# Writing the openings of four feed-forward stages out in rounds, with one plain block fewer in three of them

## The chip, the cores and the metric

The kernel runs on one core of a Trainium2 chip. The metric is the device time of one execution in microseconds. TensorE (PE in the profile, its weight loads PEld) multiplies, VectorE (DVE) and ScalarE (ACT) work element by element, GpSimd (POOL) helps them, and SyncE (SP) starts most DMAs. Each engine takes its instructions in the order in which the program issued them.

## What is computed

A trunk of two layers on 512 tokens of width 1024. Each layer is a feed-forward half step, a mixing stage, a second feed-forward half step and a gated embedding; a last norm ends it. The change touches the feed-forward half steps alone:

```python
def rmsnorm(x, g):
    y = x * lax.rsqrt(jnp.mean(x * x, axis=-1, keepdims=True) + EPS)
    return y * g

def swiglu(x, w_gate, w_up, w_down):
    return (jax.nn.silu(x @ w_gate) * (x @ w_up)) @ w_down

for i in range(DEPTH):
    h = h + 0.5 * swiglu(rmsnorm(h, ffn1_norm[i]), ffn1_w_gate[i], ffn1_w_up[i], ffn1_w_down[i])
    ...   # mixing, added to h
    h = h + 0.5 * swiglu(rmsnorm(h, ffn2_norm[i]), ffn2_w_gate[i], ffn2_w_up[i], ffn2_w_down[i])
    ...   # gated embedding, added to h
```

The weights of gate and up are 1024 x 2816, those of down 2816 x 1024.

## The kernel before

Activations lie with features on the 128 partitions and the 512 tokens along the row: `h` is eight row chunks of [128, 512]. Every f32 operand is split into a high part in the reduced format f32r (ACT, a copy) and a low part, the rest (DVE, a subtraction); one product of two operands is three matmuls, high x high, high x low, low x high (`mm3`, L160). A weight chunk is [128, 1024], eight blocks of 128 x 128.

`ffn` (L328) runs four times: FFN1 and FFN2 of layer 0, FFN1 and FFN2 of layer 1. Their first parts, up to the first products, are called the first, second, third and fourth opening below. The 22 column blocks f of gate and up are made in two ways. The first `PLAIN = 4` are plain: gate and up each take one weight chunk and 24 matmuls of 512 columns (`blocks`, L323). The other 18 go by a Strassen-like scheme in seven half-sized products (`p1` to `p7`, L511 to L600; the seven of one f are a unit), each 12 matmuls of 256 columns; their right sides are quarters of the normalised input and four combinations of them, `Th`/`Tl`, which `combined` (L404) makes once while the plain blocks run. Down (`down`, L612) comes after each group of four or five f.

The order is by hand. `item(us, run, tasks)` puts a piece of PE work on a clock of due times; its tasks (loads and splits of weights) are issued `lead` microseconds ahead of it, that is, ahead of the first item whose due time has come (L677). Inside a feed-forward stage every engine's program order is this order. In the opening:

- `chunk_tasks` (L361) loads a weight chunk (18 us ahead) and splits it (12 us ahead, two items early): the high copy on ACT, L376, then the low subtraction on DVE, L131. Raw chunks have two buffers, high and low parts three each, so the high copy of a chunk waits until PE has left the chunk three before it.
- `plain` (L425) issues the 24 matmuls of one chunk, then a step of each generator in `side`: `gated` (L393: DVE, ACT Silu, DVE, ACT, DVE for one f) and `combined` (two ACT copies `pw` L408, two POOL subtractions L411, two DVE operations L414 and L415, the ACT copy `th` L417, the DVE subtraction `tl` L131).
- `Norm.wide` (L223) makes 1/rms of all tokens on every partition at once: two matmuls with ones (L228, L229), then twelve DVE operations on [128, 512]. It stands behind the first chunk (in the first opening behind the fourth), and `gated` needs its result `st.rb`.

`Norm.tok` (L205) and `Norm.bc` (L242) are the other way, used by the mixing and embedding stages: sums of squares by token into [128, 4] (four f32 matmuls, L209, which the trace shows as eight), 1/rms on these four columns (twelve small DVE operations), then four transposes (L245) and one ACT copy (L247) to spread it over the partitions.

The stage ahead of the second and fourth opening is the mixing stage, ahead of the third the embedding stage; there the order of PE is fixed by hand or by program order and the scheduler places the other engines' work, weight splits of the coming opening among it.

Of the kernel before, what the change touches and what calls it, by code (L numbers as in the profile page):

```python
# [17 lines left out]
P = 128  # L18
# [15 lines left out]
PLAIN = 4  # L34
# [59 lines left out]
def trunk(ctx: ExitStack, tc, xT, pT, pos, W, gains, cst, dftc, out):  # L94
# [22 lines left out]
    onesr = cp.tile([P, 1], F32R, name="onesr")  # L117
    S.copy(onesr, ones)
# [61 lines left out]
    class Norm:  # L180
# [24 lines left out]
        def tok(self, by=None):  # L205

            pt = bank("pm")
# [15 lines left out]
        def wide(self, tile):  # L223

            hi, lo = tile("nhi", F32R), tile("nlo", F32R)
            split(hi, lo, self.acc)
            pt = bank("pm")
            mm(pt, onesr.to_broadcast([P, P]), hi, start=True, stop=False)  # L228
            mm(pt, onesr.to_broadcast([P, P]), lo, start=False, stop=True)  # L229
            v, a = tile("nv", F32), tile("na", F32)  # L230
            V.tensor_scalar(v, pt, 1.0 / self.n, EPS, op0=ALU.mult, op1=ALU.add)
            rb = sp.tile([P, T], F32, tag="rbc", name="rbc", bufs=3)
            g = rb.bitcast(I32)
            V.tensor_single_scalar(a.bitcast(I32), v.bitcast(I32), 1, op=ALU.arith_shift_right)
            V.tensor_scalar(g, a.bitcast(I32), -1.0, 1597463007.0, op0=ALU.mult, op1=ALU.add)
            for _ in range(3):
                V.scalar_tensor_tensor(a, rb, -0.5, rb, op0=ALU.mult, op1=ALU.mult)
                V.tensor_tensor(a, a, v, op=ALU.mult)
                V.scalar_tensor_tensor(rb, a, 1.5, rb, op0=ALU.add, op1=ALU.mult)
            return rb  # L240

        def bc(self, r, scale=1.0):  # L242
            pb = bank("pm")
# [79 lines left out]
    def blocks(o, hi, lo, st, base=0):  # L323
        for k in range(NK):
            b = slice((base + k) * P, (base + k + 1) * P)
            mm3(o, hi[:, b], lo[:, b], st.hi[k], st.lo[k], k == 0, k == NK - 1)

    def ffn(l, cgu, cd, st, nxt, first=False):  # L328
# [5 lines left out]
        with tc.tile_pool(name="ap", bufs=1) as ap, tc.manual_schedule():  # L334
# [26 lines left out]
            def chunk_tasks(w, c, halves=False, lead=12.0):  # L361

                if (l, c) in ahead:
                    w["hl"] = ahead.pop((l, c))
                    return []

                def dma():
                    w["raw"] = wp.tile([P, CHUNK], F32, tag="wraw", name="wraw", bufs=2)
                    nc.sync.dma_start(w["raw"], W[l, c])

                def prep():
                    hi = wp.tile([P, CHUNK], F32R, tag="whi", name="whi")
                    lo = wp.tile([P, CHUNK], F32R, tag="wlo", name="wlo")
                    for i in range(1 + halves):
                        b = slice(i * CHUNK // (1 + halves), (i + 1) * CHUNK // (1 + halves))
                        S.copy(hi[:, b], w["raw"][:, b])  # L376
                    lo_of(lo, w["raw"], hi)
                    w["hl"] = hi, lo
# [6 lines left out]
            side = []  # L385
# [7 lines left out]
            def gated(f, ps2):  # L393
# [9 lines left out]

            def combined(i):  # L404

                xg = tile("pw", 6, [2, T])
                for j in range(2):
                    S.activation(xg[:, j], h[:, i + 4 * j], AF.Copy, scale=st.g(i + 4 * j))  # L408
                t = tile("pw", 6, [4, H])
                (b11, b12), (b21, b22) = ((xg[:, j, 0:H], xg[:, j, H:T]) for j in range(2))  # L410
                G.tensor_tensor(t[:, 0], b11, b12, op=ALU.subtract)  # L411
                G.tensor_tensor(t[:, 1], b22, b12, op=ALU.subtract)
                yield True
                V.scalar_tensor_tensor(t[:, 2], t[:, 0], -1.0, b22, op0=ALU.mult, op1=ALU.subtract)  # L414
                V.scalar_tensor_tensor(t[:, 3], t[:, 2], -1.0, b21, op0=ALU.mult, op1=ALU.subtract)  # L415
                hi, lo = tile("th", 4, [4, H], F32R), tile("tl", 4, [4, H], F32R)
                S.copy(hi, t)  # L417
                Th.append(hi)
                Tl.append(lo)
                yield True  # L420
                lo_of(lo, t, hi)

            pairs = []

            def plain(f, i, w):  # L425
                def run():
                    n = 2 * f + i
                    if i == 0:
                        pairs.append((bank("ps"), bank("pm")))
                    blocks(pairs[f][i], *w["hl"], st)  # L430
                    if n == ready:
                        st.rb = st.norm.wide(qd)
                    late = [f] if n > ready else list(range(f + 1)) if n == ready else []
# [1123 lines left out]
```

## Time and profile before

| | us |
|---|---|
| median of 3 runs (2091.53 to 2094.8) | 2092.74 |
| the profiled execution | 2091.12 |
| its span, first to last instruction | 2089.3 |
| PE busy in the span | 2008.6 |
| DVE, ACT, POOL busy | 1567.7, 1016.6, 356.4 |
| mean granted TensorE clock | 0.985 |

The profile is of one execution. A matmul's start is recorded and its end is modelled, so the distance from one start to the next is the better measure of PE's pace. The granted clock has two levels, 1.0 (2.4 GHz) and 0.5 (1.2 GHz); a mean between them is a mixture over the stretch. An idle time in brackets is followed by the instruction that ended it.

### The profile page before, as it was taken

The page shows a single profiled execution, that of the slowest core. Times are in us where ns is not written, and L with a number is a line of the kernel's source. Part 1 is how long each engine was busy: PE and PEld are TensorE (multiplying, and loading weights), DVE is VectorE, ACT ScalarE, POOL GpSimd, SP SyncE. Part 2 cuts the span into 40 slices and gives each one's busy share as a digit, 9 for nine tenths or more (in the row PEclk, how much of TensorE's full clock was granted, in tenths as well). Part 3 has the DMA queues.
Part 4 walks back from the last instruction along what each step waited for, and adds up shares of the span by engine and source line. Part 5 has one row for each costly group of instructions (what it writes and reads, how often), then busy time and mean ns, then how long its engine had stood idle before and what let it go on. Part 6 is the DMA issues. An engine that isn't in the chain of part 4 may idle for free.

```text
span 2089.3 us, 31724 instructions
## 1 busy us (share of the span) xinstructions
PE 2008.6 (96%) x12216; PEld 1770.4 (85%) x12216; DVE 1567.7 (75%) x2607; ACT 1016.6 (49%) x1938; POOL 356.4 (17%) x415
## 2 busy tenths in 40 slices
PE   7899999999999999999999999999989999999997
PEld 5789999888777899998768999988877878999977
DVE  5687787687856778877867887776786667788777
ACT  3534454456734445445544444454675353444463
POOL 0222232001001232221011322220000022233200
PEclk9899999999999999999999999999999999999999
DMA  4365554221123555562225456522210246555431
GB/s 137 102 171 152 151 151 129 83 81 48 57 71 105 147 140 153 152 162 88 94 81 166 134 145 169 152 88 87 83 54 21 91 125 170 145 153 139 138 112 50
DMA packets 96664, 244.23 MB, mean 117 GB/s; under 512 B 10592, under 2 KB 14064, under 8 KB 96512
## 3 DMA queue, kind: packets, MB, share of 16 engines
q1 hardware_dynamic: 73488, 200.98, 28.9%
q0 software_dynamic: 20784, 37.84, 11.2%
q10 hardware_dynamic: 2240, 3.38, 0.5%
q8 instruction: 96, 1.57, 0.3%
q14 instruction: 56, 0.46, 0.1%
HBM read 240.06 MB, written 2.10 MB: 116 GB/s over the span
## 4 chain that ended last, share of the span: by engine, by line
PE 81%; DVE 8%; ACT 5%; issue 3%; DMA 1%; POOL 0%; DVEq 0%; ACTq 0%; POOLq 0%
PE ps L493 29%; PE ps L162 8%; PE ps L161 8%; PE ps L163 7%; PE pm L161 7%; PE pm L163 7%; PE pm L162 7%; PE pm L493 5%; DVE wlo L131 1%; ACT whi L376 1%; ACT pw L408 1%; DVE tl L131 1%; PE ps L718 1%; DVE xl L312 1%; PE ps L719 1%
## 5 line engine op out<-in xcount | busy, mean ns | idle before, releaser
L493 PE MATMUL ps<-th,pw 128*128 128x256 f32 x2304 | 442.9, 284 | 1.5 <-ACT pw L457 1.0
L131 DVE TENSOR_TENSOR wlo<-wraw,whi 128x1024 fp32r<-128x1024 f32 (+3 forms) x275 | 344.4, 1253 | 130.7 <-ACT whi L376 93.6
L493 PEld LDWEIGHTS ps<-th,pw 128*128 128x128 f32 x2304 | 371.6, 193 | 4.4 <-ACT pw L457 1.7
L493 PE MATMUL ps<-tl,pw 128*128 128x256 f32 x1152 | 327.1, 284 | 0.0
L376 ACT CAST whi<-wraw 128x512 fp32r<-128x512 f32 (+1 forms) x261 | 204.4, 811 | 220.9 <-PE pm L162 118.0
L493 PEld LDWEIGHTS ps<-tl,pw 128*128 128x128 f32 x1152 | 221.8, 192 | 1.1
L131 DVE TENSOR_TENSOR pw<-qd,pw 128x512 fp32r<-128x512 f32 x216 | 172.6, 801 | 9.9 <-ACT pw L457 4.8
L469 POOL DMA_DIRECT2D qd<-in_W x144 | 125.9, 963 | 215.2 <-DMA qd<-in_W 212.7
L161 PE MATMUL pm<-ah,whi 128*128 128x512 f32 x392 | 155.3, 396 | 0.0
L163 PE MATMUL pm<-ah,wlo 128*128 128x512 f32 x392 | 154.6, 394 | 0.0
L162 PE MATMUL pm<-al,whi 128*128 128x512 f32 x392 | 154.2, 393 | 0.0
L559 ACT COPY g<-ps 128x256 f32<-128x256 f32 x72 | 26.8, 373 | 231.8 <-PE ps L493 231.8
L134 ACT CAST whi<-wraw 128x1024 fp32r<-128x1024 f32 (+6 forms) x86 | 81.0, 944 | 119.4 <-PE ps L162 53.1
L161 PE MATMUL ps<-xh,whi 128*128 128x512 f32 x288 | 119.2, 414 | 18.8 <-ACT xh L305 13.6
L457 ACT CAST pw<-qd 128x512 fp32r<-128x512 f32 x216 | 124.3, 616 | 0.0
L134 ACT CAST ah<-g 128x256 fp32r<-128x256 f32 x144 | 56.7, 404 | 137.0 <-DVE g L582 130.3
L161 PE MATMUL ps<-ah,whi 128*128 128x512 f32 x312 | 123.3, 395 | 0.0
L163 PE MATMUL ps<-ah,wlo 128*128 128x512 f32 x312 | 123.0, 394 | 0.0
L162 PE MATMUL ps<-al,whi 128*128 128x512 f32 x312 | 122.7, 393 | 0.0
L131 DVE TENSOR_TENSOR pw<-qa,pw 128x512 fp32r<-128x512 f32 x144 | 108.2, 752 | 16.2 <-ACT pw L457 16.2
L163 PE MATMUL ps<-xh,wlo 128*128 128x512 f32 x288 | 117.0, 406 | 3.3 <-DVE wlo L131 3.2
L162 PE MATMUL ps<-xl,whi 128*128 128x512 f32 x288 | 117.3, 407 | 1.4 <-DVE xl L312 1.3
(389 smaller groups left out, 5187.2 us busy)
## 6 DMA issues: line engine op xcount, KB each, us to landing
wraw<-in_W SPq DMA_DIRECT2D x245, 512.0 KB, 3.4
qd<-in_W SPq DMA_DIRECT2D x216, 256.0 KB, 4.2
qd<-in_W POOLq DMA_DIRECT2D x144, 256.0 KB, 4.5
gr<-in_W SPq DMA_DIRECT2D x8, 512.0 KB, 4.0
wraw<-in_W SPq DMA_DIRECT2D x8, 320.0 KB, 2.8
wraw<-in_dftc SPq DMA_DIRECT2D x4, 516.0 KB, 3.3
h<-in_xT ACTq DMA_DIRECT2D x8, 256.0 KB, 4.4
wraw<-in_W SPq DMA_DIRECT2D x4, 408.0 KB, 3.1
```

The source lines that it names most:

```text
L131: V.tensor_tensor(lo, x, hi.bitcast(F32), op=ALU.subtract)
L134: S.copy(hi, x)
L161: mm(o, wh, xh, start=first, stop=False)
L162: mm(o, wh, xl, start=False, stop=False)
L163: mm(o, wl, xh, start=False, stop=last)
L312: V.scalar_tensor_tensor(xl, h[:, m], self.g(m), self.hi[m].bitcast(F32), op0=ALU.mult, op1=ALU.subtract)
L376: S.copy(hi[:, b], w["raw"][:, b])
L408: S.activation(xg[:, j], h[:, i + 4 * j], AF.Copy, scale=st.g(i + 4 * j))
L457: S.copy(p[:, 0], U[u][src])
L469: nc.gpsimd.dma_start(U[u][name], up[:, T:2 * T] if add == "A22" else gate[:, 0:T], accum_op=ALU.add)
L493: mm(U[u][o], x[:, b], y, start=first and i + j == 0, stop=i == 3 and j == 2, skip_group_check=not first)
L559: S.copy(d["g2"], d["B"])
```

## The change

`PLAIN` becomes 3 and `PLAIN0 = 4` is kept for the first opening (`np0` is the one that applies), so in the second to fourth opening the fourth f goes by the Strassen-like scheme. `wide`, its ones and `chunk_tasks` are removed. A class `Chunk` holds one weight chunk with `load`, `high` and `low` as separate steps (each done once), and `tasks` for the later users as before. `tok` and `bc` may be given a PSUM bank, and share one here. `combined` is cut into four: `quarters` (ACT, POOL), `combined` (DVE), `combined_high` (ACT), `combined_low` (DVE). What an item issues is written out: behind the matmuls of chunk n come the high copy of chunk n + 2 and the low subtraction of chunk n + 1 (`beside`), then a part of the combinations, then steps of `gated`. In the second to fourth opening the first two chunks are one item (`opening2`): both blocks over row chunks 0 to 6, then both over row chunk 7. The sum by token follows on PE there, and the broadcast behind chunk 2 (first opening: behind chunks 3 and 4). The core of the diff:

```diff
-PLAIN = 4
+PLAIN = 3
+PLAIN0 = 4
...
-            def chunk_tasks(w, c, halves=False, lead=12.0):
...
-                    for i in range(1 + halves):
...
-                        S.copy(hi[:, b], w["raw"][:, b])
-                    lo_of(lo, w["raw"], hi)
...
-                return [(lead + 6.0, dma), (lead, prep)]
-            ready = 3 if first else 0
+            class Chunk:
+                def load(self):
+                    if self.raw is None and self.hi is None:
+                        self.raw = wp.tile([P, CHUNK], F32, tag="wraw", name="wraw", bufs=2)
+                        nc.sync.dma_start(self.raw, W[l, self.c])
+                def high(self, n=1):
...
+                            S.copy(self.hi[:, b], self.raw[:, b])
+                def low(self):
...
+                        lo_of(self.lo, self.raw, self.hi)
...
+            np0 = PLAIN0 if first else PLAIN
...
-            def plain(f, i, w):
...
-                    if n == ready:
-                        st.rb = st.norm.wide(qd)
...
+            def beside(n):
+                if n + 2 < 2 * np0:
+                    chunks[n + 2].high()
+                if n + 1 < 2 * np0:
+                    chunks[n + 1].low()
+            def opening(n):
+                def run():
+                    plain(n)
+                    beside(n)
+                    i = n - 2
+                    if 0 <= i < 4:
+                        quarters(i)
+                    if 0 <= i - 1 < 4:
+                        combined(i - 1)
+                        combined_high(i - 1)
                     step()
+                    for f in {5: (0, 1), 6: (2,), 7: (3,)}.get(n, ()):
+                        gate(f)
+                    if 0 <= i - 1 < 4:
+                        combined_low(i - 1)
+                    if n == 3:
+                        tok()
+                    if n == 4:
+                        bc()
+            def opening2():
+                for ks in (range(NK - 1), range(NK - 1, NK)):
+                    plain(0, ks)
+                    plain(1, ks)
+                chunks[2].high()
+                chunks[2].low()
+                quarters(0)
+                quarters(1)
                 for i in range(2):
+                    combined(i)
+                    combined_high(i)
+                for i in range(2):
+                    combined_low(i)
+                tok()
+                chunks[3].high()
+            def later(n):
+                def run():
+                    plain(n)
+                    beside(n)
+                    if n == 2:
+                        quarters(2)
+                        quarters(3)
+                    if n in (2, 3):
+                        combined(n)
+                        combined_high(n)
+                    step()
+                    if n > 2:
+                        gate(n - 3)
+                    if n in (2, 3):
+                        combined_low(n)
+                    if n == 2:
+                        bc()
+            loads = lambda n: [(18.0, chunks[n].load)]
...
+                item(11.2, opening2, [(19.0, lambda: (chunks[0].load(), chunks[1].load())), (18.0, prepare)])
+                for n in range(2, 2 * np0):
+                    item(5.6, later(n), loads(n))
```

(`prepare` is `high` and `low` of chunks 0 and 1.)

## Rows read from the trace of the kernel before

**Rows 1.** Windows: busy PE, PEld, DVE, ACT, POOL (instructions), granted clock, DMA share, GB/s.

```profile
30.59:95.70 65.11, 55.04 (x256) 45.55 (x254) 42.59 (x61) 29.75 (x48) 12.12 (x14) 0.87 0.36 97
100.00:360.00 260.00, 260.00 (x1781) 241.34 (x1780) 211.46 (x325) 118.08 (x248) 70.65 (x81) 1.00 0.56 151
626.41:693.18 66.77, 62.16 (x304) 50.17 (x302) 44.64 (x64) 31.71 (x50) 11.18 (x14) 0.97 0.38 111
1046.03:1118.23 72.20, 64.88 (x304) 51.65 (x302) 50.09 (x73) 34.05 (x54) 11.19 (x14) 0.93 0.37 105
1650.72:1718.13 67.41, 63.17 (x303) 51.49 (x302) 44.65 (x64) 31.71 (x50) 11.16 (x14) 0.95 0.39 110
```

**Rows 2.** Timeline, PE, second opening: start, duration, line, out<-in [idle, releaser].

```profile
631.99 0.40 PE L228 MATMUL pm<-qd,onesr 128*128 128x512 f32 x1
...
632.45 0.39 PE L161 MATMUL pm<-xh,whi 128*128 128x512 f32 x1
...
638.02 0.39 PE L161 MATMUL ps<-xh,whi 128*128 128x512 f32 x1
```

**Rows 3.** Chain that ended last, 693 to 703 us: start, length, what.

```profile
693.34 8.62 PE ps L493 x72
```

**Rows 4.** Timeline, DVE, second opening.

```profile
632.65 0.69 DVE L231 TENSOR_SCALAR qd<-pm 128x512 f32<-128x512 f32 x1 [1.25 <-PE pm L229]
...
640.12 0.69 DVE L239 SCALAR_TENSOR_TENSOR rbc<-qd,rbc 128x512 f32<-128x512 f32 x1
```

**Rows 5.** Timeline, ACT, second opening.

```profile
641.56 0.63 ACT L396 ACTIVATE qa<-qa 128x512 f32<-128x512 f32 x1 [9.58 <-DVE qa L395]
...
657.58 1.05 ACT L417 CAST th<-pw 128x1024 fp32r<-128x1024 f32 x1 [3.28 <-DVE pw L415]
...
665.20 1.05 ACT L417 CAST th<-pw 128x1024 fp32r<-128x1024 f32 x1 [3.88 <-DVE pw L415]
```

**Rows 6.** Groups by line, shapes apart, 640 to 676 us, ACT then DVE: busy, mean ns.

```profile
L408 ACT ACTIVATE pw<-h,gv 128x512 f32<-128x512 f32 x8 | 5.3, 713 | 0.0
L376 ACT CAST whi<-wraw 128x1024 fp32r<-128x1024 f32 x5 | 5.2, 1031 | 0.0
...
L131 DVE TENSOR_TENSOR wlo<-wraw,whi 128x1024 fp32r<-128x1024 f32 x5 | 6.1, 1225 | 14.3 <-ACT whi L376 14.3
...
L415 DVE SCALAR_TENSOR_TENSOR pw<-pw 128x256 f32<-128x256 f32 x4 | 1.7, 425 | 0.1
```

**Rows 7.** Timeline, POOL, second opening.

```profile
646.41 0.75 POOL L411 TENSOR_TENSOR pw<-pw 128x256 f32<-128x256 f32 x1 [128.09 <-ACT pw L408]
```

**Rows 8.** Timeline, PE, start of the third opening.

```profile
1051.48 0.51 PE L162 MATMUL ps<-xl,whi 128*128 128x512 f32 x1 [0.54 <-DVE xl L312]
...
1054.23 0.79 PE L161 MATMUL ps<-xh,whi 128*128 128x512 f32 x1 [2.01 <-ACT xh L305]
```

**Rows 9.** Timeline, PE, around a sum by token and a broadcast in other stages.

```profile
441.01 0.95 PE L209 MATMUL pm<-ones,sqacc 128*128 128x1 f32 x8
441.82 0.48 PE L161 MATMUL ps<-xh,whi 128*128 128x512 f32 x1
...
999.36 0.62 PE L245 MATMUL pm<-cs,rtok 128*128 128x128 f32 x4
999.74 0.48 PE L161 MATMUL pm<-whi 128*128 128x512 f32 x1
```

**Rows 10.** Timeline, DVE, the twelve small steps of a 1/rms by token.

```profile
1009.33 0.15 DVE L213 TENSOR_SCALAR var<-pm 128x4 f32<-128x4 f32 x1
...
1011.51 0.16 DVE L177 SCALAR_TENSOR_TENSOR rtok<-rs_a,rs_y 128x4 f32<-128x4 f32 x1
```

**Rows 11.** The page, part 6: DMA issues, KB each, median us to landing.

```profile
qd<-in_W POOLq DMA_DIRECT2D x144, 256.0 KB, 4.5
```

**Rows 12.** Windows: a stretch with both of Rows 9's kinds, and one with idle PE.

```profile
442.00:454.00 12.00, 12.00 (x55) 9.73 (x55) 11.16 (x30) 9.79 (x16) 0.00 (x0) 1.00 0.13 44
665.00:675.00 10.00, 8.48 (x29) 6.11 (x29) 6.13 (x9) 5.31 (x7) 4.01 (x5) 0.83 0.56 127
```

More of the change, by code (lines that the diff above doesn't have):

```diff
@@ L221, in tok, with bc @@
             return r
[L223 to L243, printed above, removed]
+        def bc(self, r, scale=1.0, pb=None):
+            pb = bank("pm") if pb is None else pb
             for c in range(NT):
@@ L321, in bc, with blocks @@
             self.rb = self.norm.bc(self.rt)
-    def blocks(o, hi, lo, st, base=0):
-        for k in range(NK):
+    def blocks(o, hi, lo, st, base=0, ks=range(NK)):
+        for k in ks:
             b = slice((base + k) * P, (base + k + 1) * P)
@@ L419, in combined @@
-                Tl.append(lo)
-                yield True
-                lo_of(lo, t, hi)
-            pairs = []
-            def plain(f, i, w):
-                def run():
[L427 to L430, printed above, removed]
-                    if n == ready:
-                        st.rb = st.norm.wide(qd)
-                    late = [f] if n > ready else list(range(f + 1)) if n == ready else []
-                    step()
-                    i0 = n - (2 if first else 1)
-                    if 0 <= i0 < 4:
-                        side.append(combined(i0))
-                        next(side[-1])
-                    if i == 0 or n == ready:
-                        for x in late:
-                            side.append(gated(x, pairs[x]))
-                            next(side[-1])
-                return run
@@ L446, in ffn, with combined @@
-            for f in range(PLAIN):
-                for i in range(2):
-                    w = {}
-                    tasks = chunk_tasks(w, cgu + 2 * f + i)
-                    item(5.6, plain(f, i, w), tasks)
+            def combined(i):
+                xg, t = xgs.pop(i), ts[i]
+                V.scalar_tensor_tensor(t[:, 2], t[:, 0], -1.0, xg[:, 1, H:T], op0=ALU.mult, op1=ALU.subtract)
+                V.scalar_tensor_tensor(t[:, 3], t[:, 2], -1.0, xg[:, 1, 0:H], op0=ALU.mult, op1=ALU.subtract)
@@ new lines, in combined_high, with combined_low, gate, tok @@
+            def combined_high(i):
+                Th.append(tile("th", 4, [4, H], F32R))
+                S.copy(Th[i], ts[i])
+            def combined_low(i):
+                Tl.append(tile("tl", 4, [4, H], F32R))
+                lo_of(Tl[i], ts.pop(i), Th[i])
+            def gate(f):
+                side.append(gated(f))
+                next(side[-1])
+            pairs = []
+            chunks = [Chunk(cgu + n) for n in range(2 * np0)]
+            norm_bank = []
+            def tok():
+                norm_bank.append(bank("pm"))
+                st.rt = st.norm.tok(pt=norm_bank[0])
@@ new lines, in ffn, with prepare @@
+            loads = lambda n: [(18.0, chunks[n].load)]
+            if first:
+                for n in range(2 * np0):
+                    item(5.6, opening(n), loads(n))
+            else:
+                def prepare():
+                    for n in range(2):
+                        chunks[n].high()
+                        chunks[n].low()
+                item(11.2, opening2, [(19.0, lambda: (chunks[0].load(), chunks[1].load())), (18.0, prepare)])
+                for n in range(2, 2 * np0):
+                    item(5.6, later(n), loads(n))
@@ L521, in run @@
                     step()
-                return run, chunk_tasks(U[u]["gate"], cgu + 2 * u, True, 10.1)
+                return run, U[u]["gate"].tasks(2, 10.1)
             def p5(u):
@@ L638, in ffn @@
             SL = 1.434
-            put(SL, p1(PLAIN))
-            put(SL, p5(PLAIN))
-            put(SL, p2(PLAIN))
+            put(SL, p1(np0))
+            put(SL, p5(np0))
+            put(SL, p2(np0))
             g, f0 = 0, 0
-            for u in range(PLAIN, NF - 1):
-                prev = u - 1 if u > PLAIN else None
+            for u in range(np0, NF - 1):
+                prev = u - 1 if u > np0 else None
                 put(SL, p6(u))
```

76 lines of the change are left out of this document (41 added, 35 removed).

## The prediction

> **What bounds the kernel now.** I read the windows first, then PE's timeline in the stretches where it loses time, then the timelines of the engines that it waits for there. PE is the bound: in a steady feed-forward stretch it is busy for 260.00 of 260.00 us, with DVE at 211 and ACT at 118 [rows 1]. A plain block of 24 matmuls takes 5.57 us (632.45 to 638.02) and the two matmuls of `wide` 0.46 (631.99 to 632.45) [rows 2]; 72 half-width matmuls take 8.62, so a product of twelve takes 1.44 [rows 3]. The other stretches of [rows 1] are the four openings, each from its first plain matmul (the first opening: from its third block, since the blocks before that wait for the inputs) to the end of the second `p2`, nine products in. PE's own work there is 8 x 5.57 + 0.46 + 9 x 1.437 = 57.95 us (first: 6 blocks, 46.81). What is above that is lost: 65.11 - 46.81 = 18.3 in the first opening, 66.77 - 57.95 = 8.8 in the second, 72.20 - 57.95 = 14.3 in the third, 67.41 - 57.95 = 9.5 in the fourth, together 50.8 us [rows 1].
>
> **Why it is lost there.** Two things. `wide` holds DVE from 632.65 to 640.81 [rows 4], and ACT, in order, sits 9.58 us before a Silu that needs its result [rows 5], with the high copy of a later weight chunk queued behind. After that the laps are too long: from one `th` copy to the next takes 665.20 - 657.58 = 7.62 us [rows 5] against 5.57 for the block, because ACT and DVE pass the work to and fro. The lap, by the mean times [rows 6]: two `pw` copies 1.43, high copy 1.03, low part 1.22, `tl` 1.22 (same shape), two operations of L415's kind 0.85, `th` 1.05 [rows 5], 6.8 in all, and the gating of one f makes up the rest. DVE idles 14.3 us in that stretch for the high copies alone [rows 6]: neither engine is full, the order is the bound. The third opening also waits at its start for the last row chunks, 2.01 us in one place [rows 8], and half clock follows the idle: 0.83 granted over ten microseconds is 1.7 us of PE time [rows 12].
>
> **The change part by part.**
>
> *1/rms by token.* It takes twelve wide DVE steps (8.2 us [rows 4]) off and puts twelve small ones there, 1009.33 to 1011.67, 2.3 us [rows 10]. PE pays: 0.81 for the sum (441.01 to 441.82) and 0.38 for the transposes (999.36 to 999.74) [rows 9], less 0.46 for `wide`: +0.73 each, four times +2.9 us. It adds one wait on PE: the transposes stand ahead of the next block in PE's queue and need DVE's last small step. ACT gets one copy of 512 columns (at most the 0.71 of L408 [rows 6]), one more link ahead of the first gate.
>
> *Rounds.* In the new order the low part of chunk n + 1 needs a high copy that ACT made a round earlier, so the lap is cut in two. I count the second opening from its first plain matmul. PE: two blocks to 11.1, the sum to 11.9, block 2 to 17.5, transposes to 17.9, block 3 to 23.5, block 4 to 29.0, block 5 to 34.6. ACT first has a high copy and the last row chunk's two copies (to about 2.3, at the prices of [rows 6]), then the quarters 0 and 1 to 5.1; POOL takes 1.5 for each pair [rows 7]; the two `th` copies end near 8.4, the lows near 9.7. DVE then stands before the sum, which comes at 11.9, and the small steps end at 14.3, wanted at 17.5: 3.2 to spare. The low part of chunk 3 comes at 15.5, wanted (third matmul of its block) at 18.4; chunk 4's behind the third combination at 19.8, wanted at 24.0; chunk 5's at 24.0, wanted at 29.5; the first Strassen chunk's at 27.9, wanted at 34.6. So nothing is late, and the cover is 3 to 7 us; where it is gone, each microsecond costs one. The high copy of chunk 3 waits for block 0, whose last use is now three matmuls from the end of the pair (10.4 instead of 5.6): it lands at 11.5, long before 17.9. In the first opening the same counting leaves 3 us for the transposes and over 4 for the later chunks. The gating there starts two blocks later (behind chunk 5) and shares DVE with the last splits: about 5.1 us of DVE work in that round by the prices of [rows 6], against 5.57.
>
> *Loads.* Raw chunks keep two buffers, so on SP's queue the load of chunk 5 waits for the low part of chunk 3 (15.5), and the first Strassen operand S1 is queued behind it. S1 lands at about 20 and POOL's accumulating DMA behind it at 25 to 26, with 4.5 for each [rows 11]; wanted at 30. That is 4 us of cover; POOL's two subtractions for quarters 3 are issued before it.
>
> *Two blocks share their row chunks.* No matmul is added. In the third opening row chunk 6 is still in the first sweep: PE is there 18 matmuls in, at 1050.2, and its second matmul, due at 1050.4, began at 1051.48 [rows 8]; this 1.0 us stays. Row chunk 7, there at 1054.2 [rows 8], is now wanted at about 1056.9: hidden. But ACT's combinations start some 6 us later than in the second opening, so that the small steps end about when block 2 does, and chunk 3's low part may be a few tenths late. I put 2 us for this opening, 0.5 for each other, 3.5 in all. The bounds: nothing, or, where the scheduler puts the quarters' four copies (2.9 us [rows 6]) ahead of the last row chunk on ACT, 1.0 + 2.9 + 1.7 for the clock [rows 12], 5.6 in that opening.
>
> *One plain block fewer.* Two blocks, 11.14 us, become seven products, 10.06: -1.08, three times -3.2 us. The added unit's splits and loads lie beside PE as those of the steady stretch do, where PE loses nothing [rows 1]; at worst they cost what one lap is too long, 7.62 - 5.57 = 2.05 each [rows 5].
>
> *The start.* One tiny ACT copy (the ones) goes; PE waits for inputs there, so nothing, within two copies either way (1.4 [rows 6]).
>
> **The sum.** Losses 50.8 + 3.2 - 2.9 = 51.1 at most; less 3.5 left over: 47.6. The profiled execution took 2091.12 (span 2089.3 and 1.8 around it) and becomes 2043.5; the median of the runs shown is 1.6 above it, so I predict 2045.
>
> **The rivals.**
>
> *The laps stay.* If ACT and DVE still wait for each other once a round, four rounds of each opening run at 7.62 instead of 5.57: 8.2 each, 32.8 in all, and the gain is 51.1 - 32.8 = 18.3: 2074. For it: the chain quarters, POOL, DVE, ACT, DVE is as long as before. Against: only its own last step waits for all of it; the weight splits no longer do, and the lists above have 3 to 7 us of cover.
>
> *The third opening stays stuck.* Its start keeps the 5.6 worked out above, the transposes wait a further 2 or so in the three openings where DVE has the combinations ahead of them: about 11 left over, 2053. For it: there ACT gets the last row chunks late; against: row chunk 7 has 2.7 us.
>
> *The clock falls at the small matmuls.* The trace keeps 1.00 over a stretch with a sum by token and four transposes [rows 12]. The Trainium skill, page "TensorE: Matmul & The Clock Gate", section "Part 4: PE-mode transpose", says that a transpose does not count as PE work in the same way and that full clock does not engage for it; each opening now has four of them. By that rule a half-clock stretch would follow in each opening; the trace disagrees [rows 12]. One stretch of half clock in each, like the one of 1.7 us in [rows 12], would give 4 x 1.7 = 6.8 more: 2052.
>
> *Slower.* The same mechanism, if PE stayed at half clock from the sum by token to the last plain block: four blocks of 5.57 in each opening take twice as long, 4 x 22.3 = 89 more: 2092.7 - 51.1 + 89 = 2131. It decides from 51.1 / 4 = 12.8 us at full-clock pace run at half in each opening. Against it: 1.00 in [rows 12], and 0.87 at the lowest over a whole opening even with today's waits [rows 1].
>
> **How the numbers follow.** Forecast (2041 to 2050) 0.72; third opening stuck 0.10; laps stay 0.10; clock falls once per opening 0.03; slower 0.03; no change, the laps longer than before, 0.02. About 0.2% (4 us) is what a measurement of this kernel can tell from no change. Faster 0.95, same 0.02, slower 0.03. The range runs from 2039 (all of the 51.1, and the start's 1.4 on the good side) to 2062: it takes in the forecast, the stuck opening and the clock, 0.85, and part of the way to the laps; 2074 is left out.
>
> **What would show it.** Right: between `wide`'s old place and the first product no PE idle over 0.5 us but at the third opening's row chunk 6; windows from the first plain matmul to the second `p2` of 6 x 5.57 + 1.19 + 12.93 = 47.5 us, plus 0.5 to 2, in the second to fourth opening; the granted clock 1.00 there. Wrong: PE waits before the transposes or for low parts, ACT idle of several microseconds before `th` with high copies behind it, or Strassen operands S1 that land late.

## The result, and the profile after

The changed kernel took 2042.28 us (median of 4 runs, 2039.42 to 2044.95), the kernel before 2093.34 beside it (2091.53 to 2094.8). The ratio is 0.9767, 95% interval 0.9753 to 0.978, so about 49 us faster by the ratio; the two medians lie 51.1 us apart. 2045 had been forecast, with 2039 to 2062 as the range. The profiled execution of after is the slowest of its four, 2044.95 with a span of 2043.2. One execution in the whole study, the profiled one of `subs_on_dve` below, ran at 1.28 us a 512-column matmul from start to end instead of 0.232, so it stands in no comparison, and only durations of DVE and what ran beside them are read from its trace.

The openings of after, as windows (busy PE, PEld, DVE, ACT, POOL with instructions, granted clock, DMA share, GB/s). They answer [rows 1], and the second to fourth now end at the second `p2` of a stage that has one plain f less:

```profile
29.21:78.18 48.97, 48.18 (x265) 41.35 (x264) 35.99 (x58) 28.99 (x46) 11.61 (x14) 1.00 0.48 130
611.79:659.53 47.74, 47.74 (x266) 41.25 (x264) 37.89 (x57) 28.89 (x46) 12.89 (x15) 1.00 0.54 152
1024.25:1073.86 49.61, 48.40 (x266) 41.04 (x265) 41.57 (x65) 30.22 (x47) 12.23 (x15) 1.00 0.52 145
1615.18:1662.65 47.47, 47.47 (x265) 41.06 (x264) 37.90 (x57) 28.48 (x45) 13.23 (x15) 1.00 0.55 150
```

The forecast for the second to fourth was 47.5 plus 0.5 to 2 at a clock of 1.00. In the second and fourth PE is busy for every microsecond of the window. Against [rows 1], less the 10.06 us of the seven products that the later unit moves out of the window, the gains are 65.11 - 48.97 = 16.1, 66.77 - 47.74 - 10.06 = 9.0, 72.20 - 49.61 - 10.06 = 12.5 and 67.41 - 47.47 - 10.06 = 9.9, together 47.5 us; 47.6 had been forecast. By opening the forecast was 17.1, 8.7, 12.7 and 9.4 (the loss there, less 0.73, plus 1.08 where a plain f goes, less what I left over). The rest of the span gave 47.5 - (2089.3 - 2043.2) = 1.4 back. The stretch before the first opening became 1.4 shorter (30.59 to 29.21) and the long stretches between and after the openings together 2.8 longer, for reasons that I have not followed.

The waits of PE in the first and the third opening (engine, line, releaser: us, times, longest) are all that the two windows list; in the second and fourth there is none:

```profile
PE ps L562 <- ACT g L628: 0.8, 1, 0.8
...
PE pm L225 <- DVE rtok L176: 1.1, 1, 1.1
```

The laps of ACT in the second opening, which answer [rows 5]:

```profile
617.66 1.05 ACT L415 CAST th<-pw 128x1024 fp32r<-128x1024 f32 x1 [1.25 <-DVE pw L411]
619.00 1.05 ACT L415 CAST th<-pw 128x1024 fp32r<-128x1024 f32 x1 [0.29 <-DVE pw L411]
...
630.37 1.05 ACT L415 CAST th<-pw 128x1024 fp32r<-128x1024 f32 x1 [3.71 <-DVE pw L411]
...
634.70 1.05 ACT L415 CAST th<-pw 128x1024 fp32r<-128x1024 f32 x1 [0.17 <-DVE pw L411]
```

The laps of before are gone: the copies come in pairs, 1.3 and 4.3 us apart. In before there are three laps between the four copies, 7.02, 7.62 and 7.02 us; the first and the last copy, with those of [rows 5] between them, are:

```profile
650.56 1.05 ACT L417 CAST th<-pw 128x1024 fp32r<-128x1024 f32 x1 [2.74 <-DVE pw L415]
...
672.22 1.05 ACT L417 CAST th<-pw 128x1024 fp32r<-128x1024 f32 x1 [3.28 <-DVE pw L415]
```

DVE's idle for high copies of weight chunks, 14.3 us in [rows 6], is 1.9 us from 611.79 to 646.6:

```profile
L130 DVE TENSOR_TENSOR wlo<-wraw,whi 128x1024 fp32r<-128x1024 f32 x5 | 6.1, 1222 | 1.9 <-ACT whi L360 1.9
```

One thing in the trace I had not counted. The small steps of 1/rms, 2.3 us in [rows 10], took 4.4 us here, 623.92 to 628.35. First DVE's timeline, then POOL's, then ACT's, of the same microseconds:

```profile
624.72 0.16 DVE L174 TENSOR_TENSOR rs_a<-rs_a,var 128x4 f32<-128x4 f32 x1
624.92 0.75 DVE L176 SCALAR_TENSOR_TENSOR rs_y<-rs_a,rs_g 128x4 f32<-128x4 f32 x1
625.70 0.66 DVE L173 SCALAR_TENSOR_TENSOR rs_a<-rs_y 128x4 f32<-128x4 f32 x1
...
628.18 0.17 DVE L176 SCALAR_TENSOR_TENSOR rtok<-rs_a,rs_y 128x4 f32<-128x4 f32 x1
...
624.90 0.74 POOL L404 TENSOR_TENSOR pw<-pw 128x256 f32<-128x256 f32 x1 [6.73 <-ACT pw L401]
625.60 0.75 POOL L405 TENSOR_TENSOR pw<-pw 128x256 f32<-128x256 f32 x1
...
624.11 2.56 ACT L401 ACTIVATE pw<-h,gv 128x512 f32<-128x512 f32 x4
```

Each of four steps that met a subtraction of POOL ended when that subtraction did: 624.92 + 0.75 = 625.67 beside 624.90 + 0.74 = 625.64, and 625.70 + 0.66 = 626.36 beside 625.60 + 0.75 = 626.35. ACT's copies are not what holds them: they run from 624.11, and the steps from there to 624.88 still take 0.16 to 0.17 us. In the third opening the chain took 4.3 us, 1038.81 to 1043.06, and PE waited for it.

### The profile page after: what moved, and what is told of

It reads as the page before. It is cut to its first block, busy times and chain, and to the rows that moved or that the text cites. A ratio compares the mean times of both kernels' runs of the same rounds, so it can differ in the third digit from the quotient of the medians.

```text
span 2043.2 us, 32106 instructions
## 1 busy us (share of the span) xinstructions
PE 1987.2 (97%) x12364; PEld 1767.7 (87%) x12364; DVE 1571.1 (77%) x2630; ACT 1027.4 (50%) x1967; POOL 373.0 (18%) x430
## 4 chain that ended last, share of the span: by engine, by line
PE 86%; DVE 7%; ACT 3%; issue 2%; DMA 1%; POOL 0%; DVEq 0%; ACTq 0%; POOLq 0%; SPq 0%
PE ps L562 30%; PE ps L161 8%; PE ps L160 8%; PE ps L162 8%; PE pm L160 7%; PE pm L161 7%; PE pm L162 7%; PE pm L562 5%; DVE wlo L130 1%; DMA wraw<-in_W 1%; DVE xl L292 1%; PE ps L787 1%; PE ps L789 1%; PE ps L788 1%; DVE sqacc L198 1%
## 5 line engine op out<-in xcount | busy, mean ns | idle before, releaser
L562 PE MATMUL ps<-th,pw 128*128 128x256 f32 x2400 | 457.4, 283 | 0.9 <-ACT g L628 0.8
L130 DVE TENSOR_TENSOR wlo<-wraw,whi 128x1024 fp32r<-128x1024 f32 (+6 forms) x272 | 344.5, 1267 | 76.0 <-ACT whi L133 37.9
L562 PEld LDWEIGHTS ps<-th,pw 128*128 128x128 f32 x2400 | 384.6, 191 | 2.6 <-ACT g L628 1.0
L562 PE MATMUL ps<-tl,pw 128*128 128x256 f32 x1200 | 339.2, 283 | 0.0
L562 PEld LDWEIGHTS ps<-tl,pw 128*128 128x128 f32 x1200 | 229.6, 191 | 1.1
L130 DVE TENSOR_TENSOR pw<-qd,pw 128x512 fp32r<-128x512 f32 x225 | 181.0, 804 | 14.9 <-ACT pw L526 9.7
L130 DVE TENSOR_TENSOR pw<-qa,pw 128x512 fp32r<-128x512 f32 x150 | 114.5, 763 | 13.2 <-ACT pw L526 13.2
L160 PE MATMUL ps<-xh,whi 128*128 128x512 f32 x264 | 107.8, 409 | 12.4 <-ACT xh L285 11.7
L562 PE MATMUL ps<-xh,pw 128*128 128x256 f32 x600 | 119.9, 283 | 0.0
L573 POOL TENSOR_TENSOR g<-g,c 128x256 f32<-128x256 f32 x75 | 65.0, 867 | 282.3 <-ACT g L572 282.3
```

The costliest lines, as they stand in the source:

```text
L130: V.tensor_tensor(lo, x, hi.bitcast(F32), op=ALU.subtract)
L160: mm(o, wh, xh, start=first, stop=False)
L562: mm(U[u][o], x[:, b], y, start=first and i + j == 0, stop=i == 3 and j == 2, skip_group_check=not first)
L573: G.tensor_tensor(d["g2"], d["g2"], d["c22"], op=ALU.mult)
```

## The experiments

Each is timed against the kernel before, on the chip that it ran on. To set them side by side, each ratio is turned into a difference from 2092.74 us:

| kernel | median, us | ratio, 95% interval | difference, us |
|---|---|---|---|
| the change | 2042.28 | 0.9767 (0.9753 to 0.978) | -48.8 |
| token_only | 2075.72 | 0.9924 (0.9907 to 0.9942) | -15.9 |
| plain3_only | 2107.96 | 1.0079 (1.0064 to 1.0094) | +16.5 |
| token_plain3 | 2088.87 | 0.9992 (0.9982 to 1.0001) | -1.7 |
| wide_back | 2067.24 | 0.9886 (0.9871 to 0.99) | -23.9 |
| plain4 | 2054.06 | 0.9828 (0.9814 to 0.9841) | -36.0 |
| plain4_late | 2052.02 | 0.9812 (0.9798 to 0.9827) | -39.3 |
| one_each | 2050.55 | 0.9807 (0.9793 to 0.982) | -40.4 |
| one_each_old | 2062.24 | 0.986 (0.9846 to 0.9875) | -29.3 |
| low_two | 2047.06 | 0.9786 (0.9768 to 0.9805) | -44.8 |
| apart | 2044.43 | 0.9782 (0.9769 to 0.9795) | -45.6 |
| quarters_early | 2040.26 | 0.9764 (0.9751 to 0.9778) | -49.4 |
| subs_on_dve | 2039.88 | 0.9758 (0.9743 to 0.9773) | -50.6 |

### One part alone, in the old order

**token_only**: the kernel before with 1/rms by token.

```diff
...
-                        st.rb = st.norm.wide(qd)
+                        norm_bank.append(bank("pm"))
+                        st.rt = st.norm.tok(pt=norm_bank[0])
+                    if n == ready + 1:
+                        st.rb = st.norm.bc(st.rt, pb=norm_bank[0])
...
```

The start of each f's gating moves with it, behind the broadcast.

> The kernel before with 1/rms by token alone: sum behind the first chunk (first opening: the fourth), broadcast one chunk later, gates behind that; four plain blocks, order otherwise as before. Theory (two causes, the wide steps and laps of ACT and DVE that are too long): laps start some 5 us earlier, so about half of each opening's loss goes, and 2.9 us of PE are added: 2075 (2068 to 2082). Rival (the wide steps were the whole cause): all but the 6.6 us at the start of the third opening goes, 2052.

Measured: 15.9 us off, a third of the whole. The laps stay: in the second opening `th` copies of ACT stand 8.15, 7.62 and 7.03 us apart. The middle one:

```profile
647.51 1.05 ACT L419 CAST th<-pw 128x1024 fp32r<-128x1024 f32 x1 [3.88 <-DVE pw L417]
655.13 1.06 ACT L419 CAST th<-pw 128x1024 fp32r<-128x1024 f32 x1 [3.88 <-DVE pw L417]
```

So `wide` was one cause and the laps another, as the prediction had it.

**plain3_only** and **token_plain3**: the same edit of the number of plain f, on the kernel before and on `token_only`.

```diff
-PLAIN = 4
+PLAIN = 3
+PLAIN0 = 4
...
-            for f in range(PLAIN):
+            np0 = PLAIN0 if first else PLAIN
+            for f in range(np0):
...
```

> The kernel before with three plain blocks in the second to fourth opening and nothing else. Theory (the combinations are bound by the laps of ACT and DVE, not by the number of blocks): PE comes to the first product that needs them two blocks earlier and waits there; slower by 3 to 6 us in each of three openings: 2105 (2100 to 2112). Rival (the swap is worth its PE time wherever it is made): 3.2 us faster, 2090.

> The kernel before with 1/rms by token and three plain blocks in the second to fourth opening; order as before, first two blocks apart. What is left to the changed kernel is the rounds and the shared row chunks. Theory: the combinations still come at laps of about 7.6 us and are wanted two blocks earlier, so the swap gains nothing: 2078 (2070 to 2085). Rival (the parts add up): 3.2 below the kernel with the sum by token alone.

Measured: 16.5 us slower alone, and beside 1/rms by token it takes back 14 of the 15.9 us. With two blocks less the late operands meet the products: PE's waits of `plain3_only` from 650 to 690 us, the window of its nine products behind the blocks, and the waits of `token_plain3` (of each kernel's four waits the two longest; the 4.9 us lie ahead of the window):

```profile
PE ps L495 <- ACT whi L377: 4.9, 1, 4.9
PE ps L495 <- DVE tl L132: 2.1, 1, 2.1
```

```profile
665.92:688.80 22.88, 18.17 (x108) 17.06 (x109) 16.42 (x24) 10.32 (x21) 5.20 (x6) 0.68 0.63 150
```

```profile
PE ps L498 <- ACT pw L462: 2.6, 1, 2.6
PE ps L498 <- DVE tl L132: 2.1, 1, 2.1
```

Nine products need 12.93 us [rows 3]; here they take 22.88, part of it idle, and the granted clock is 0.68 over the window. I had the direction of the first. For `token_plain3` I had said that the edit gains nothing; it costs 14 us, and the time came out 11 us above what was expected and outside its range: 22.85 us for the same nine products of its second opening (657.27 to 680.12), at a granted clock of 0.78. Each tenth of clock missing there is 2.3 us of PE.

### One part taken back out of the change

**wide_back**: the change with `wide` in place of the sum by token and the broadcast.

```diff
...
-                tok()
+                st.rb = st.norm.wide(qd)
                 chunks[3].high()
...
```

> The changed kernel with 1/rms of all tokens at once (wide) in the place of the sum by token, and no broadcast behind it. Theory (the twelve wide DVE steps, 8.2 us, stand in front of the low part of chunk 3, in the first opening of chunk 5): low part of chunk 3 about 3.6 us late in the second and fourth opening, about 6 in the third, of chunk 5 about 3.7 in the first; less 0.73 per opening for PE and the waits that are there now: 2055 (2052 to 2060). Rival (the order of the rounds alone does it, DVE has room for the wide steps): PE saves 4 x 0.73, 2039.

Measured: 24.9 us slower than the change, twice what I had counted. PE's wait in the second opening and DVE ahead of it:

```profile
628.29 1.11 DVE L238 SCALAR_TENSOR_TENSOR qd<-rbc 128x512 f32<-128x512 f32 x1
...
636.39 1.22 DVE L132 TENSOR_TENSOR wlo<-wraw,whi 128x1024 fp32r<-128x1024 f32 x1
...
637.66 0.74 PE L164 MATMUL pm<-xh,wlo 128*128 128x512 f32 x1 [5.00 <-DVE wlo L132]
```

The low part of chunk 3 stands behind the twelve wide steps. Four of those ran beside POOL at 1.11 to 1.12 us instead of 0.69, so they took 9.8 us where [rows 4] gave 8.2, and half clock follows the wait (a granted clock of 0.75 from 637.66 to 644.45 in the second opening). The block behind `wide` lost 5.9, 6.8 and 7.1 us in the first, second and fourth opening; in the third it lost 6.7, and 5.5 more went at `wide` and in the block ahead. `wide` costs more here than in the old order (24.9 us against 15.9). That this is because a low part is made one block ahead of its use, not two, is argued from the order and was not run by itself.

**apart**: the first two blocks one after the other.

```diff
-                for ks in (range(NK - 1), range(NK - 1, NK)):
-                    plain(0, ks)
-                    plain(1, ks)
+                plain(0)
+                plain(1)
```

> The changed kernel with the first two blocks of the second to fourth opening one behind the other, over all eight row chunks each. Theory: only the third opening waits for row chunk 7, about 2.7 us, and gives back the 1.5 that it now waits before and behind the transposes; the others don't change: 2043.5 (2042 to 2046). Rival (the shared sweep is what took the third opening's start loss of 6.6 us): 2049.

Measured: 3.2 us above the change by the ratios, whose intervals overlap, near the first of the two expectations. In the third opening PE waits for the last two row chunks again, 2.0 us for one and 0.3 for the other:

```profile
PE ps L160 <- ACT xh L285: 2.0, 1, 2.0
```

**low_two**: the low part of a weight chunk in the round of its high copy.

```diff
                 if n + 2 < 2 * np0:
                     chunks[n + 2].high()
-                if n + 1 < 2 * np0:
-                    chunks[n + 1].low()
+                    chunks[n + 2].low()
...
                 chunks[3].high()
+                chunks[3].low()
```

> The changed kernel with the low part of a chunk made in the same round as its high copy, two chunks ahead, instead of one chunk ahead. Reason given in the prediction (the low part one round behind the high copy is what cuts the lap): laps go back towards 7.6 us, 2 us a round, 2055 to 2070. Rival (the lap is cut by the rest: no wide steps, gates behind the combinations, combinations in parts): DVE waits a little for each high copy and nothing reaches PE, 2042.3 within 2.

Measured: 2047.06, 4 us above the change by the ratios, whose intervals overlap, and not the 2055 to 2070 that the prediction's reason asked for, nor within 2 of 2042.3 as the other expectation had it. `th` copies come 1.34 and 4.74 us apart (617.83 and 619.17, 631.67 and 636.41). So the low part's being a round behind its high copy is not by itself what cut the laps, and `one_each` and `one_each_old` below find what did.

**plain4** and **plain4_late**: four plain f everywhere; `plain4` begins the gating of the fourth f behind chunk 6, `plain4_late` behind chunk 7 (the edit shown is that of `plain4_late`).

```diff
-PLAIN = 3
+PLAIN = 4
...
-                    if n > 2:
-                        gate(n - 3)
+                    for f in {3: (0,), 4: (1,), 5: (2,), 7: (3,)}.get(n, ()):
+                        gate(f)
```

> The changed kernel with four plain blocks in all openings (gates of f = 0 to 3 behind chunks 3 to 6). Theory (in the new order neither form leaves PE waiting, so the swap is worth its PE time): 3 x 1.08 us slower, 2045.5 (2044 to 2047.5). Rival (the fewer blocks are themselves what took waits away): 2050 or more.

> The changed kernel with four plain f everywhere, and the gating of the fourth begun behind the last block (chunk 7) instead of behind chunk 6. In plain4 the nine products after each of the second to fourth opening took 14.4 us instead of 12.9: at 656 us ACT's copy for the last f's activations stood ahead of its copy for the second Strassen operand. Theory: that order is the cause, and with it mended three more plain blocks cost 3 x 1.08 = 3.2 us alone: 2045.5 (2044 to 2048), nine products in 12.9 to 13.1 us in the second to fourth opening. Rival: the products are late behind eight blocks whatever the order: 2050 or more, as plain4 had it (2054).

Measured: 12.8 and 9.5 us above the change, where 3.2 was counted for three swaps. A part of `plain4` was of my making. Its ACT, at the end of the second opening's blocks, and the product that waited:

```profile
655.95 0.62 ACT L394 CAST ah<-qa 128x512 fp32r<-128x512 f32 x1 [3.91 <-DVE qa L392]
656.48 0.61 ACT L526 CAST pw<-qd 128x512 fp32r<-128x512 f32 x1
...
657.14 0.39 PE L562 MATMUL ps<-th,pw 128*128 128x256 f32 x1 [0.54 <-ACT pw L526]
```

The copy `ah` of the last f needs the last block and stands ahead of the copy of a product's operand. With the gating one round later that copy comes first, 4 us ahead of the last block's end (658.43):

```profile
654.33 0.61 ACT L526 CAST pw<-qd 128x512 fp32r<-128x512 f32 x1
...
660.31 0.62 ACT L394 CAST ah<-qa 128x512 fp32r<-128x512 f32 x1
```

and the 1.5 us that the nine products lost in each opening are gone, though the medians moved by 2 to 3 us only. In the traces of the change and of `plain4_late` the six blocks more (33.4 us) and the three shorter stretches of products (29.7 us) make 3.7 of the 9.6 us between the spans. The other 5.9 lie outside, in the stages between and at the end, where half clock is granted for longer (49 us in all against 38, at most 5 us of PE). Why is open. The price of the three plain f more is 3.7 by these stretches, where 3.2 was counted, and 8 to 10 by the medians of `one_each` and `plain4_late`.

### What cut the laps

**one_each**: `plain4_late` with the combinations one a round, as before; the low part of a weight chunk stays a round behind its high copy. **one_each_old**: the same, with the low part in the round of its high copy, which is the old order.

```diff
...
+                    if 0 <= n - 3 < 4:
+                        combined_low(n - 3)
+                    if 0 <= n - 2 < 4:
+                        combined(n - 2)
+                        combined_high(n - 2)
                     step()
+                    if 0 <= n - 1 < 4:
+                        quarters(n - 1)
...
```

> plain4_late, but in the second to fourth opening the four combinations are made one a round as in the kernel before (quarters i, a round later combination i and its high copy, a round after that its low part, each behind the next weight chunk's low part on DVE); the low part of a weight chunk stays one round behind its high copy. Theory of the prediction (the low part a round behind its high copy is what cuts the laps): no lap is over 5.57 us, PE loses nothing in the blocks: 2045 to 2048, as plain4_late. Rival (making the combinations two at once, with their low parts in the same round, is what cut them): laps near 7.6 us again, one to four of them showing in each of three openings: 2055 to 2070.

> one_each, with the low part of a weight chunk in the round of its high copy (two chunks ahead), which is the kernel before's order of combinations and splits in the second to fourth opening; 1/rms by token and the shared row chunks stay. Theory (either of the two parts alone cuts the laps, both gone bring them back): a lap of high copy 1.03, low 1.14, low of a combination 1.14, two operations 0.85, its high copy 1.05, two quarter copies 1.3 and a gating's two copies 1.1 = 7.6 us, 2.05 over a block, over four rounds, less what the head start covers: 4 to 8 us for each of three openings over plain4_late: 2057 to 2070, with th copies 7.6 us apart. Rival (the order of splits and combinations is not what set the laps; 1/rms by token and the shared row chunks did it all): as plain4_late, 2045.5.

Measured: `one_each` equals `plain4_late` (0.9807 and 0.9812), PE loses nothing in its second opening. `one_each_old` is 11 us slower than `one_each`. ACT's copies of the second opening, `one_each` and then `one_each_old` with one row of its DVE and the waits of its PE:

```profile
630.89 1.05 ACT L415 CAST th<-pw 128x1024 fp32r<-128x1024 f32 x1 [0.74 <-DVE pw L411]
...
635.96 1.04 ACT L415 CAST th<-pw 128x1024 fp32r<-128x1024 f32 x1
...
641.30 1.05 ACT L415 CAST th<-pw 128x1024 fp32r<-128x1024 f32 x1 [1.06 <-DVE pw L411]
```

```profile
635.94 1.05 ACT L415 CAST th<-pw 128x1024 fp32r<-128x1024 f32 x1 [3.27 <-DVE pw L411]
...
644.38 1.06 ACT L415 CAST th<-pw 128x1024 fp32r<-128x1024 f32 x1 [3.28 <-DVE pw L411]
...
651.92 1.05 ACT L415 CAST th<-pw 128x1024 fp32r<-128x1024 f32 x1 [3.28 <-DVE pw L411]
...
648.68 1.23 DVE L130 TENSOR_TENSOR wlo<-wraw,whi 128x1024 fp32r<-128x1024 f32 x1 [3.19 <-ACT whi L360]
```

```profile
PE ps L555 <- DVE wlo L130: 1.3, 1, 1.3
...
```

With both gone the laps are back, 8.4 and 7.5 us, and DVE idles 3.2 us for the high copy, then works off `wlo`, `tl` and two operations while ACT idles 3.3. With the low part a round behind, DVE starts at once and the lap is 5.1 and 5.3. With two combinations at once and their low parts in the same round (`low_two`) there are half as many laps. In the second to fourth opening either one is enough; the change has both. (`low_two` has three plain f there, the other kernels of this comparison four.) In the second and fourth opening `one_each_old` takes as long as `token_only`, 62.75 and 62.88 us, 63.45 and 63.05, from the first plain matmul to the second `p2`, so the two parts account there for what the order gives.

The first opening is another matter. `one_each_old` has the low part in the round of its high copy there too, and in every kernel written in rounds the first opening makes one combination a round; yet it is as short as in the change. Its windows, `token_only` and then `one_each_old`, counted as in [rows 1]:

```profile
28.05:86.15 58.10, 51.54 (x265) 43.94 (x264) 37.05 (x61) 29.72 (x48) 12.62 (x14) 0.91 0.38 109
...
28.93:77.42 48.49, 47.95 (x266) 41.26 (x265) 38.02 (x58) 29.09 (x46) 12.85 (x14) 1.00 0.45 131
```

Of the 16.1 us that the first opening gained, 1/rms by token gives 65.11 - 58.10 = 7.0, and about 9 come from the rest of the new order. In the rounds a combination's low part stands in the round of its own high copy and the gating starts one chunk later than in `token_only`; whether one of these or something else in the order does it, no run shows.

### Small steps beside POOL

**quarters_early**: quarters 2 and 3 issued in the first item, ahead of the sum by token.

```diff
...
                 quarters(1)
+                quarters(2)
                 for i in range(2):
                     combined(i)
                     combined_high(i)
+                quarters(3)
...
```

> The changed kernel with the quarters 2 and 3 made ahead of the sum by token (second to fourth opening), so that no POOL subtraction runs beside the small DVE steps. Theory (a small DVE step with two operands in SBUF waits out a POOL subtraction: 0.66 us each instead of 0.16): the steps take 2.4 us in all three openings instead of up to 4.4, and PE's wait of 1.2 us before the transposes of the third opening goes: 2040.8 (2039.5 to 2042.5). Rival (the steps are slow for another reason): steps of 0.66 stay, 2042.3.

Measured: 2040.26, not told apart from the change. In the second opening, where no subtraction runs beside the small steps, the chain takes 2.3 us, and in the fourth as well. Its first and last step in the second:

```profile
621.89 0.16 DVE L212 TENSOR_SCALAR var<-pm 128x4 f32<-128x4 f32 x1 [1.76 <-PE pm L208]
...
624.07 0.16 DVE L176 SCALAR_TENSOR_TENSOR rtok<-rs_a,rs_y 128x4 f32<-128x4 f32 x1
```

In the third opening PE still waits 0.83 us before the transposes. POOL's subtractions only met other work of DVE there (the two `tl` parts took 2.89 us together, where two of 1.22 follow each other elsewhere, and two other small steps became slow):

```profile
1032.95 2.89 DVE L130 TENSOR_TENSOR tl<-pw,th 128x1024 fp32r<-128x1024 f32 x2
...
1035.95 0.52 DVE L167 TENSOR_SCALAR rs_i<-var 128x4 int32<-128x4 int32 x1
1036.50 0.67 DVE L169 TENSOR_SCALAR rs_g<-rs_i 128x4 int32<-128x4 int32 x1
```

**subs_on_dve**: the subtractions of quarters 2 and 3 on DVE, behind the small steps.

```diff
...
-                        quarters(2)
-                        quarters(3)
+                        quarters(2, False)
+                        quarters(3, False)
                     if n in (2, 3):
+                        differences(n, V)
                         combined(n)
...
```

> The changed kernel, but the four subtractions for quarters 2 and 3 in the second to fourth opening run on DVE, ahead of the two operations that need them, instead of on POOL. Theory: the small 1/rms steps took 4.4 us (second opening) and 3.8 us (third) instead of 2.3 because POOL's subtractions ran beside them; with POOL idle there every step takes 0.15 to 0.2 us again, the chain 2.3 to 2.5 us, and PE's wait before the transposes of the third opening (1.23 us) and the 0.36 us behind it go: 2040.6 (2039 to 2043), for DVE has 1.7 us more in that round but spare time. Rival: the steps are slow for another reason (the PSUM read, the ACT copies beside them): they stay at 0.65 us beside ACT's copies, the wait stays, 2042.3.

Measured: 2039.88, the lowest of all; its interval overlaps that of the change, so a gain of 1.8 us is not shown. Its trace agrees with the mechanism. One group of small steps over the whole program (busy, mean ns), first of this kernel, then of the change:

```profile
L176 DVE SCALAR_TENSOR_TENSOR rs_y<-rs_a,rs_g 128x4 f32<-128x4 f32 x14 | 2.3, 162 | 0.5
```

```profile
L176 DVE SCALAR_TENSOR_TENSOR rs_y<-rs_a,rs_g 128x4 f32<-128x4 f32 x14 | 3.9, 281 | 0.4
```

No small step is slow where POOL does not read beside it. This trace alone would not settle it, since ACT has no work beside the small steps of its openings either; the change's own rows and `quarters_early` do. Whether PE's wait in the third opening goes with it can't be read from that execution.

## Why the prediction was right, step by step

*What bounds the kernel, and the 50.8 us.* Right. The second and fourth opening now lose nothing, and the gain in the four windows is 47.5 of the 47.6 forecast.

*1/rms by token.* The direction and PE's price held: 0.81 and 0.36 us for the two groups of small matmuls. DVE's price was mis-sized: the small steps took 4.4 us, not the 2.3 of [rows 10], because those rows stand where POOL is idle and the new place is beside its subtractions. The low part of chunk 3 ended at 629.5, 17.7 after the start of the window instead of 15.5, wanted at 18.5. About 0.8 us was left of the cover that I had put at 2.9, so nothing was lost in the second and fourth opening. The forecast of 3 to 7 us of cover was too good.

*Rounds.* The outcome was right, the reason half of it. "In the new order the low part of chunk n + 1 needs a high copy that ACT made a round earlier, so the lap is cut in two": `one_each` shows that this is enough. `low_two` shows that it is not needed, because the change also makes the combinations two at once. I had the pair in my own count (both `th` copies ended near 8.4, the lows near 9.7; in the trace 8.3 and 9.5) and did not see that it cuts the laps as well. Neither accounts for the first opening, where about 9 us went by the order without them; that part of the forecast came out without its reason. The lap of 7.62 that I priced was also the longest of before's three, 7.02, 7.62 and 7.02, so the rival's four rounds at 7.62 were priced too high.

*Loads.* Nothing came late, but most of the cover that I had counted went. S1 landed 22.3 us after the start of the second opening instead of 20, and POOL's accumulating DMA behind it, one of three with a median of 6.9 us there instead of 4.5, at 29.0 instead of 25 to 26. That is 1 us ahead of the 30 that I had put and 3.9 ahead of ACT's copy, which began at 32.9.

*Third opening.* The sum of 2 us was right (49.61 less 47.5), its places were not, so that the sum agrees is luck. The 1.0 us at row chunk 6 did not come: its low part landed 4.3 us after the opening's start, where PE could go on only after 5.45 in before [rows 8]. DVE's batch of six low parts ahead of it began 3.4 us before the opening instead of 2.3. Before, then after:

```profile
1043.77 4.06 DVE L312 SCALAR_TENSOR_TENSOR xl<-h,gv,xh 128x512 fp32r<-128x512 f32 x6
...
1020.87 4.06 DVE L292 SCALAR_TENSOR_TENSOR xl<-h,gv,xh 128x512 fp32r<-128x512 f32 x6
...
1027.79 0.75 DVE L292 SCALAR_TENSOR_TENSOR xl<-h,gv,xh 128x512 fp32r<-128x512 f32 x1
```

PE, due there at 1028.6, did not stop. Instead 1.1 us went at the transposes, a sign that the text had given to a rival, 0.3 at the low part of chunk 3 behind them, and 0.4 in the products:

```profile
1043.11 0.65 PE L225 MATMUL pm<-cs,rtok 128*128 128x128 f32 x4 [1.06 <-DVE rtok L176]
```

*First opening.* 16.1 against 17.1. The 1.3 us that its products lose at 72.3 us wait for an ACT copy behind the last f's gating, the same order that `plain4` showed; I had said that nothing is late there.

*One plain block fewer.* -3.2 was the price with every operand in time, and the openings of `plain4_late` bear it out (3.7); its median says 9.5, and where the rest comes from is open. `plain3_only` shows what the sentence left out: in the old order the same edit costs 16.5 us. It pays only once the laps are short, so it is no term of its own.

*The rivals.* The laps did not stay. The clock did not fall at the small matmuls: each opening has four transposes and the granted clock is 1.00 over all four windows, so the rule of the Trainium skill ("TensorE: Matmul & The Clock Gate", "Part 4: PE-mode transpose") gives nothing here; with it both the 2052 and the 2131 fall. The window that I read for it, [rows 12], begins at 442.00 and so holds four transposes but not the sum by token, which ended at 441.82 [rows 9]; the stretch with the sum is at 1.00 too:

```profile
436.00:442.00 6.00, 6.00 (x32) 5.03 (x31) 4.81 (x8) 1.59 (x4) 0.00 (x0) 1.00 0.27 90
```

The third opening lost 2 us and not 11. Not slower: no cover was overrun by more than 1.3 us.

## What to carry to other kernels

Where two engines pass work to and fro, write the order so that each step needs something made a round earlier, or make two pieces in one pass; in three of the four openings here either broke the lap, and the gain is seen in the idle of both engines and not in anyone's busy time. Parts of a change don't add: three plain f fewer, worth 3 to 10 us once the operands are early, cost 16 while they were late, so cost each part in the order that it will stand in. Take the price of a small operation from a row with the same neighbours: beside another engine's reads of SBUF it may last as long as they do.

## What the runs showed of the hardware

A DVE step on 4 columns takes 0.16 us, and 0.52 to 0.75 us when it meets a POOL subtraction of 0.74 us; it then ends when POOL's instruction does. Four of the twelve wide steps in `wide_back`, beside POOL's four subtractions, took 1.11 to 1.12 us instead of 0.69, and three of those subtractions 1.18 to 1.19. The Trainium skill ("SBUF — State Buffer", "Who interferes with whom") says that a DVE instruction with two SBUF inputs contends with a GpSimd instruction that reads SBUF; that whoever issues first holds the shared ports for its whole instruction, and the other blocks, it says of DVE's two-port modes. The rows agree with the first and look like the second, and show also that one small step is held for each subtraction, so that twelve steps of 2.3 us became 4.4 us beside four subtractions. Two of the slow steps in `quarters_early` (L167, L169) are of the tensor-scalar kind with one input; the Trainium skill counts that kind only in the two-port modes, and no row shows which mode they ran in.
